# The decays of a group's scan computed at the end of the round before, in a decoder block on one core

## The chip, the cores and the metric

The kernel runs on one core of one Trainium2 chip. The metric is the device time of one execution in microseconds (us); smaller is better. Before the change three runs gave 1035.84, 1035.08 and 1036.63 us, median 1035.84.

## The reference

One layer of a hybrid decoder on 512 tokens with 16 learned meta tokens ahead of them, width 1024, in float32. A large input projection feeds two branches, a causal pooling and a Mamba-2 state-space scan (SSD). Sigmoid gates merge them, an output projection and a squared-ReLU MLP follow. The change lies in the scan, which has 8 groups of 4 heads and chunks of 128 positions:

```python
a_cs = jnp.cumsum(a_dt, axis=2)
diff = a_cs[:, :, :, None] - a_cs[:, :, None, :]
lmat = jnp.exp(jnp.where(mask, diff, -jnp.inf))
cb = jnp.einsum("bclgn,bcsgn->bclsg", cf, bf)
y_diag = jnp.einsum("bclsg,bclsgr,bcsgrp->bclgrp", cb, lmat, xdt)
...
y_off = jnp.einsum("bclgn,bcgrpn,bclgr->bclgrp", cf, prev, jnp.exp(a_cs))
...
y = y.reshape(bsz, seqlen, D_INNER) * jax.nn.silu(z)
yg = yg * lax.rsqrt(jnp.mean(yg * yg, axis=-1, keepdims=True) + EPS)
```

The "decays" are the two exponentials: `exp(a_cs)` (tile `eb`) and `lmat` (computed in place in tile `abc`, also called `dm`). The norm in the last line needs the sum of the squares of `y` (tile `sqg`).

## The kernel before, in words

Weights come in blocks of 128x1024 floats. Each is loaded by SyncE into `raw` (3 buffers), cast by ScalarE (ACT) to a rounded `whi` (L75) and completed by VectorE (DVE) with `wlo`, the rest (L76; 4 buffers each); every product is then three matmuls on TensorE (PE). Blocks are made two ahead of their use.

The scan goes in rounds g = 0 to 7. Round g runs `ssd(g)` (L398) and, between its parts, as filler for PE, the projections of group g+1 (`group_proj`, L364): `bt`, `ct`, two halves `xc`, in some rounds a gate (`pgp`, L537), and two halves of `z` (`pz`). `weave` (L524) interleaves the two by counts; PE's order is what this writing gives, while the order on ACT, DVE and the DMA queues is made by a scheduler. All engines take their instructions strictly in the order that results.

A round in PE's order, with the default counts: transposes of the group (`ptb`, `ptm`, `ptx`, L413 to L434); projection `bt`; `pcb` and the chunk states `pst` (L461 to L470); projection `ct`; projection of the first `xc`; the outputs `po` and `py` (L485, L491), called **the end of py** below; projection of the second `xc`; gate and both `pz`; the norm's column sums `png` (L508). In round 3 `STEPS` puts `png` ahead of `pz`. Round 4 has as filler first the eight half tiles `pso` of the output product (`out_half`, L569), each copied to `acc` by ACT (L574); two halves share a PSUM tile, and the second half's first matmul waits for the copy of the first. Round 7's filler is `psp` (`out_part`, L577), which needs group 6's normed rows `yh`, `yl` (L519, L520).

What ACT and DVE do for a round: the decays. POOL issues the load of `abc` (L406: four rows of `acs_d` sent to all 128 partitions, 1 MB), as soon as the `py` of the round before has read the single `abc` buffer. Then ACT makes two `eb` (L445: exp of half the partitions each), eight Relu of `abc` (L450) while DVE makes eight differences (L453), and ACT two exponentials of 128x1024 (L455, L456). Further: copies of the transposes to `btok`, `bm` (L415 to L420), and for each projection ACT's first convolution tap (L344), three taps on DVE (L347) and a Silu on ACT (L349); only the taps release the projection's PSUM tile, of which there are two (`psum2`). Then `yt` on DVE (L495 to L499), its square on ACT (L503, `sqg`, which shares the buffer of `eb`), a sum on DVE, `qhg` on ACT (L246) and `qlg` on DVE (L247) for `png`, Ln and Exp on ACT (L511, L512), the scaled rows (L516) and their split `yh`, `yl`. ACT holds one table of functions at a time: a change between Exp, Silu, Sigmoid and Ln puts an ACT_TABLE_LOAD into its order.

Of the kernel before, what the change touches and what calls it, by code (L numbers as in the profile page):

```python
# [9 lines left out]
F32 = mybir.dt.float32  # L10
F32R = mybir.dt.float32r
AF = mybir.ActivationFunctionType
ALU = mybir.AluOpType

P = 128
D = 1024
SEQ = 512
# [4 lines left out]
G = 8  # L22
R = 4
# [28 lines left out]
def kernel(ctx: ExitStack, tc, xT, x, w, vec, fnw, out):  # L52
    nc = tc.nc
    act, dve, pe, pool = nc.scalar, nc.vector, nc.tensor, nc.gpsimd
# [66 lines left out]
    dtok = const.tile([P, 2, 4, HEADS], F32, name="dtok")  # L121
# [16 lines left out]
    for i in range(2):  # L138
        dve.tensor_scalar(xm[:, 2 * i : 2 * i + 2, :].rearrange("p r d -> p (r d)"), ones_f[:MQ], 0.0, None,
                          op0=ALU.mult)  # L140
# [6 lines left out]
    def psum1(name):  # L147
        return psb.tile([P, 512], F32, tag="s", name=name)
# [93 lines left out]
    def col_sums(name, qt, n2, tags, bufs=1):  # L242

        qh = n2.tile(list(qt.shape), F32R, tag=tags[0], name=f"qh{name}", bufs=bufs)
        ql = n2.tile(list(qt.shape), F32R, tag=tags[1], name=f"ql{name}", bufs=bufs)
        act.copy(qh, qt)  # L246
        dve.tensor_tensor(ql, qt, qh.bitcast(F32), op=ALU.subtract)  # L247
        return qh, ql
# [20 lines left out]
    for i in range(2):  # L269
        pb = psum1(f"pb1_{i}")  # L270
        c = slice(3 * i, 3 * i + 3)
# [14 lines left out]
    for c in range(4):  # L286
        r = slice(c * H, (c + 1) * H)
# [23 lines left out]
    acs_d = dram.tile([H, SEQ], F32, name="acs_d")  # L311
# [39 lines left out]
    def group_tiles(g):  # L351
        xc = gc.tile([P, 2, L], F32, tag="xc", name=f"xc{g}")
        bt = gc.tile([P, L], F32, tag="bt", name=f"bt{g}")
        ct = gc.tile([P, SEQ], F32, tag="ct", name=f"ct{g}")
        zt = gc.tile([P, 2, SEQ], F32, tag="zt", name=f"zt{g}", bufs=1)
        return xc, bt, ct, zt
# [7 lines left out]
    def group_proj(g, cur, gate=None):  # L364

        first = g == 0
        xc, bt, ct, zt = cur
        for dst, t, skip in ((bt, 16 + g, 0), (ct, 24 + g, NM - 4), (xc[:, 0, :], 2 * g, 0),
                             (xc[:, 1, :], 2 * g + 1, 0)):
            if first and dst is bt:  # L370
                view = viewB
            else:
                runs, view = wide(psum2(f"px{g}_{t}"), skip)
                proj(runs, block(), X if first else U)
            conv(dst, first_raw(t, view, skip) if first else view, t)
            yield
        if gate is not None:
            gate_pool(gate)
            yield
        ps = psum2(f"pz{g}")  # L380
        for i in range(2):
            proj(narrow(ps[:, i * SEQ : (i + 1) * SEQ]), block(), X if first else U)
            if gate is None and i == 0:
                yield
        zf = zt.rearrange("p i t -> p (i t)")
        if first:
            dve.tensor_tensor(zt, ps.rearrange("p (i t) -> p i t", i=2),
                              rsb[:, NM:].unsqueeze(1).to_broadcast([P, 2, SEQ]), op=ALU.mult)
            act.activation(zf, zf, AF.Silu)
        else:  # L390
            act.activation(zf, ps, AF.Silu)
        yield


    def bc(ap, n):
        return ap.unsqueeze(len(ap.shape)).to_broadcast(list(ap.shape) + [n])

    def ssd(g, cur):  # L398

        xc, bt, ct, zt = cur  # L400
        hs = slice(R * g, R * g + R)
        tok = lambda c: slice(NM + c * P, NM + (c + 1) * P)
        ctok = lambda c: slice(c * P, (c + 1) * P)
        flat = lambda t: t.rearrange("p r d -> p (r d)")
        abc = gs.tile([P, R, SEQ], F32, tag="abc", name=f"abc{g}")
        nc.gpsimd.dma_start(abc, acs_d[hs, :].partition_broadcast(P))  # L406

        xdt = gs.tile([P, 4, R, 64], F32, tag="xdt", name=f"xdt{g}")
        xdm = gs.tile([NM, R, 64], F32, tag="xdm", name=f"xdm{g}")
        btok = gs.tile([P, 3, P], F32, tag="btok", name=f"btok{g}")  # L410
# [27 lines left out]
        xdd = gs.tile([P, 3, R, 64], F32, tag="xdd", name=f"xdd{g}")  # L438
        dve.tensor_tensor(xdd, xdt[:, :3, :, :], bc(dec[:, :3, hs], 64), op=ALU.mult)

        eb = gs.tile([P, 2, SEQ], F32, tag="eb", name=f"eb{g}")
        ap = abc.rearrange("p (i j) l -> p i j l", j=2)
        for j in range(2):
            js = slice(64 * j, 64 * j + 64)
            act.activation(eb[js, :, :], ap[js, :, j, :], AF.Exp)  # L445
        dm = abc.rearrange("p r (c l) -> p r c l", c=4)
        for r in range(R):
            for c in range(4):
                if r < 2:
                    act.activation(dm[:, r, c, :], dm[:, r, c, :], AF.Relu, scale=-1.0,  # L450
                                   bias=dtok[:, 1, c, R * g + r : R * g + r + 1])
                else:
                    dve.tensor_scalar(dm[:, r, c, :], dm[:, r, c, :], dtok[:, 1, c, R * g + r : R * g + r + 1],  # L453
                                      0.0, op0=ALU.subtract, op1=ALU.min)
        act.activation(abc[:, :2], abc[:, :2], AF.Exp, scale=-1.0)  # L455
        act.activation(abc[:, 2:], abc[:, 2:], AF.Exp)  # L456
        yield

        pc = psum1(f"pcb{g}")
# [27 lines left out]
        for i in range(2):  # L487
            for c in range(4):
                for j in range(2):
                    r = 2 * i + j  # L490
                    pe.matmul(py[i][64 * j : 64 * j + 64, c * P : (c + 1) * P],  # L491
                              xdt[:, c, r, :], dm[:, r, c, :], start=True, stop=True)
        for i in range(2):
# [4 lines left out]
                                     op0=ALU.mult, op1=ALU.add)  # L498
            dve.tensor_tensor(y, y, zt[:, i, :], op=ALU.mult)  # L499
            if i == 0:  # L500
                yield
        sq = gs.tile([P, 2, SEQ], F32, tag="eb", name=f"sqg{g}")
        act.activation(sq, yt, AF.Square)  # L503
        dve.tensor_tensor(sq[:, 0, :], sq[:, 0, :], sq[:, 1, :], op=ALU.add)
        qh, ql = col_sums(f"g{g}", sq[:, 0, :], gs, ("qh", "ql"))
        yield
        pn = psum1(f"png{g}")
        pe.matmul(pn, ones_r, qh, start=True, stop=False)  # L508
# [15 lines left out]
    def weave(a, b, counts):  # L524

        end = object()
        for _, n in zip(a, counts):
            while n and b:
                if next(b[0], end) is end:
                    b.pop(0)  # L530
                else:
                    n -= 1
        for rest in [a] + b:
            for _ in rest:
                pass
# [18 lines left out]
    gs = gc_stack.enter_context(tc.tile_pool(name="gs", bufs=1, side="left", reuse_waits="tile"))  # L554
# [14 lines left out]
    def out_half():  # L569
        for dd in range(4):  # L570
            ps = psum2(f"pso{dd}")
            for i in range(2):
                ssd_out(2 * dd + i, ps[:, i * SEQ : (i + 1) * SEQ], range(8))
                act.copy(acc[2 * dd + i], ps[:, i * SEQ : (i + 1) * SEQ])  # L574
                yield

    def out_part():  # L577

        un = units()
        for d in range(NK):  # L580
            ps = psum2(f"psp{d}")[:, :SEQ]
            for k in range(8, 14):
                mm3(ps, next(un), ys[k], k == 8, k == 13)
            dve.tensor_tensor(acc[d], acc[d], ps, op=ALU.add)
            yield

    STEPS = {3: (1, 1, 1, 1, 1, 1, 0), 4: (2, 2, 2, 2, 2, 4, 0), 7: (2, 2, 0, 2, 1, 1, 0)}
    depth[0] = 2
    with tc.manual_schedule(engines={mybir.EngineType.PE}):
        for g in range(G):  # L590
            nxt = group_tiles(g + 1) if g + 1 < G else None
            fill = [group_proj(g + 1, nxt, GATE_AT.get(g))] if nxt else [out_part()]
            if g == 4:
                fill = [out_half()] + fill
            weave(ssd(g, cur), fill, STEPS.get(g, (1, 1, 1, 1, 2, 0, 0)))
            cur = nxt
# [161 lines left out]
    for n, d in enumerate(MERGE):  # L758
# [8 lines left out]
        for i, k in enumerate(ks):  # L767
            c = slice(k * P, (k + 1) * P)
# [294 lines left out]
    c = NC - 1  # L1063
# [5 lines left out]
    for t in range(4):  # L1069
        T, st = t // 2, slice((t % 2) * P, (t % 2 + 1) * P)  # L1070
        n = 0
        for half in range(2):
            parts = [(0, 512)] if half == 0 or t < 3 else [(0, 256), (256, 256)]
            for a, m in parts:
# [3 lines left out]
                i = 0  # L1078
                for k, seg in ((1, (A11, 3)[T]), (0, (A12, A22)[T])):
                    wh, wl = wq[k, half]  # L1080
                    for p in range(2):
                        x0 = p * 512 + a
                        f = i == 0 and not (T == 0 and half == 0)
# [152 lines left out]
```

## Time and profile before

| | |
|---|---|
| median of 3 runs | 1035.84 us |
| the profiled execution, its own time | 1034.4 us |
| its span, first to last instruction | 1032.7 us |
| PE busy | 1007.3 us (98%) |
| DVE busy | 714.5 us (69%) |
| ACT busy | 562.7 us (54%) |
| mean granted TensorE clock | 0.993 |

A row of the timeline gives start and duration in us, engine, line, operation and tiles; in brackets stands the idle time of the engine before it and whose end released it. "PEclk" is the share of the full TensorE clock that was granted.

### The profile page before, as it was taken

The page shows a single profiled execution, that of the slowest core. Times are in us where ns is not written, and L with a number is a line of the kernel's source. Part 1 is how long each engine was busy: PE and PEld are TensorE (multiplying, and loading weights), DVE is VectorE, ACT ScalarE, POOL GpSimd, SP SyncE. Part 2 cuts the span into 40 slices and gives each one's busy share as a digit, 9 for nine tenths or more (in the row PEclk, how much of TensorE's full clock was granted, in tenths as well). Part 3 has the DMA queues.
Part 4 walks back from the last instruction along what each step waited for, and adds up shares of the span by engine and source line. Part 5 has one row for each costly group of instructions (what it writes and reads, how often), then busy time and mean ns, then how long its engine had stood idle before and what let it go on. Part 6 is the DMA issues. An engine that isn't in the chain of part 4 may idle for free.

```text
span 1032.7 us, 14079 instructions
## 1 busy us (share of the span) xinstructions
PE 1007.3 (98%) x5689; PEld 874.0 (85%) x5689; DVE 714.5 (69%) x950; ACT 562.7 (54%) x748; POOL 88.6 (9%) x52
## 2 busy tenths in 40 slices
PE   9999999999889999989999999999999999999997
PEld 8888889898678898968899888888888888888886
DVE  7988676776535585967756457875777567666866
ACT  7774959577526629582334333374554345454444
POOL 0100000000000000000000000002131422403400
PEclk9999999999899999999999999999999999999999
DMA  6243141423322231413532333324323323233112
GB/s 236 73 156 105 34 148 41 144 62 128 97 76 109 87 118 42 144 37 106 205 102 83 104 100 100 125 82 146 100 82 122 105 92 110 102 103 123 41 42 82
DMA packets 29281, 105.62 MB, mean 102 GB/s; under 512 B 3296, under 2 KB 4256, under 8 KB 28192
## 3 DMA queue, kind: packets, MB, share of 16 engines
q1 hardware_dynamic: 26496, 92.75, 27.7%
q0 software_dynamic: 2000, 11.08, 2.8%
q8 instruction: 44, 0.72, 0.3%
q10 hardware_dynamic: 720, 0.91, 0.3%
q14 instruction: 21, 0.17, 0.1%
HBM read 102.55 MB, written 2.16 MB: 101 GB/s over the span
## 4 chain that ended last, share of the span: by engine, by line
PE 82%; ACT 9%; DVE 6%; issue 2%; DMA 1%; SPq 0%; ACTq 0%; DVEq 0%
PE pf L96 6%; PE pf L98 6%; PE pf L97 6%; PE px L154 4%; PE px L155 4%; PE px L157 4%; PE alpha L985 3%; PE alpha L987 3%; PE alpha L986 3%; PE pz L154 2%; PE pz L157 2%; PE pz L155 2%; PE pp L157 1%; PE pp L154 1%; PE pp L155 1%
## 5 line engine op out<-in xcount | busy, mean ns | idle before, releaser
L76 DVE TENSOR_TENSOR wlo<-raw,whi 128x1024 fp32r<-128x1024 f32 (+1 forms) x131 | 163.3, 1252 | 146.8 <-ACT whi L75 146.8
L75 ACT CAST whi<-raw 128x1024 fp32r<-128x1024 f32 (+1 forms) x131 | 135.7, 1043 | 219.2 <-PE pf L97 55.8
L154 PE MATMUL px<-uh,whi 128*128 128x264 f32 (+1 forms) x448 | 120.2, 289 | 4.1 <-DVE bt L347 2.5
L155 PE MATMUL px<-ul,whi 128*128 128x264 f32 (+1 forms) x448 | 117.3, 283 | 0.0
L96 PE MATMUL pf<-vh,whi 128*128 128x512 f32 x256 | 99.8, 390 | 0.0
L98 PE MATMUL pf<-vh,wlo 128*128 128x512 f32 x256 | 99.6, 389 | 0.0
L97 PE MATMUL pf<-vl,whi 128*128 128x512 f32 x256 | 99.6, 389 | 0.0
L157 PE MATMUL px<-uh,wlo 128*128 128x264 f32 (+1 forms) x448 | 90.4, 283 | 0.0
L154 PEld LDWEIGHTS px<-uh,whi 128*128 128x128 f32 x448 | 84.7, 189 | 5.7 <-issue 3.7
L155 PEld LDWEIGHTS px<-ul,whi 128*128 128x128 f32 x448 | 84.4, 188 | 0.2
L747 DVE TENSOR_TENSOR slo<-b,shi 128x1024 fp32r<-128x1024 f32 x35 | 49.2, 1404 | 31.6 <-ACT shi L746 31.6
L157 PEld LDWEIGHTS px<-uh,wlo 128*128 128x128 f32 x448 | 68.8, 188 | 0.0
L746 ACT CAST shi<-b 128x1024 fp32r<-128x1024 f32 x35 | 36.8, 1050 | 47.3 <-PE pf L97 36.4
L98 PEld LDWEIGHTS pf<-vh,wlo 128*128 128x128 f32 x256 | 48.1, 188 | 10.0
L97 PEld LDWEIGHTS pf<-vl,whi 128*128 128x128 f32 x256 | 48.1, 188 | 10.0
L96 PEld LDWEIGHTS pf<-vh,whi 128*128 128x128 f32 x256 | 48.1, 188 | 9.8
L996 POOL TENSOR_TENSOR b<-b,b 128x1024 f32<-128x1024 f32 x14 | 35.5, 2539 | 238.3 <-DVE slo L747 238.3
L985 PE MATMUL alpha<-shi,hh 128*128 128x512 f32 x140 | 54.6, 390 | 0.0
L987 PE MATMUL alpha<-shi,hl 128*128 128x512 f32 x140 | 54.5, 389 | 0.0
L986 PE MATMUL alpha<-slo,hh 128*128 128x512 f32 x140 | 54.5, 389 | 0.0
L812 DVE TENSOR_TENSOR ht<-ht,alpha 128x1024 f32<-128x1024 f32 x35 | 42.6, 1217 | 10.9 <-PE alpha L987 10.9
L154 PE MATMUL pz<-uh,whi 128*128 128x512 f32 x112 | 44.0, 392 | 1.8 <-DVE xc L347 1.4
(419 smaller groups left out, 2497.8 us busy)
## 6 DMA issues: line engine op xcount, KB each, us to landing
raw<-in_w SPq DMA_DIRECT2D x129, 512.0 KB, 3.5
b<-in_w SPq DMA_DIRECT2D x28, 512.0 KB, 3.5
abc<-acs_d POOLq DMA_DIRECT2D x8, 1024.0 KB, 5.6
wob<-in_w SPq DMA_DIRECT2D x8, 512.0 KB, 5.2
xt<-in_xT SPq DMA_DIRECT2D x8, 264.0 KB, 5.9
ht<-in_x POOLq DMA_DIRECT2D x4, 512.0 KB, 6.2
w<-in_w SPq DMA_DIRECT2D x4, 512.0 KB, 3.5
out_dram<-out SPq DMA_DIRECT2D x4, 320.0 KB, 2.4
```

The lines of the kernel that those rows point to most:

```text
L75: act.copy(hi[:, c], raw[:, c])
L76: dve.tensor_tensor(lo[:, c], raw[:, c], hi[:, c].bitcast(F32), op=ALU.subtract)
L96: pe.matmul(ps, ah, bh, start=first, stop=False)
L97: pe.matmul(ps, ah, bl, start=False, stop=False)
L98: pe.matmul(ps, al, bh, start=False, stop=last)
L154: pe.matmul(o, wh, rhs[0][k][:, c], start=k == 0, stop=False)
L155: pe.matmul(o, wh, rhs[1][k][:, c], start=False, stop=False)
L157: pe.matmul(o, wl, rhs[0][k][:, c], start=False, stop=k == NK - 1)
L747: dve.tensor_tensor(lo, src, hi.bitcast(F32), op=ALU.subtract)
L985: pe.matmul(ps[t], a[0], wh[:, cs], start=f, stop=False, skip_group_check=True)
L986: pe.matmul(ps[t], a[0], wl[:, cs], start=False, stop=False, skip_group_check=True)
L987: pe.matmul(ps[t], a[1], wh[:, cs], start=False, stop=l, skip_group_check=True)
```

## The change

Five edits. The decays get a function of their own, `decays(g)`: load, `eb`, differences, exponentials. Group 0's are called ahead of the rounds. Those of group g+1 are called in round g after the norm's squares and `col_sums`, ahead of `png`; before, they stood in round g+1 between the transposes and `pcb`. The squares `sqg` get a buffer of their own, `sq`, so that `eb` of the next group can be written while they are in use. `STEPS` has a new entry for round 6, which puts `png` between the two halves of `pz`.

```diff
+    decay = {}
+    def decays(g):
+        hs = slice(R * g, R * g + R)
+        abc = gs.tile([P, R, SEQ], F32, tag="abc", name=f"abc{g}")
+        nc.gpsimd.dma_start(abc, acs_d[hs, :].partition_broadcast(P))
+        dm = abc.rearrange("p r (c l) -> p r c l", c=4)
+        eb = gs.tile([P, 2, SEQ], F32, tag="eb", name=f"eb{g}")
...
+        act.activation(abc[:, :2], abc[:, :2], AF.Exp, scale=-1.0)
+        act.activation(abc[:, 2:], abc[:, 2:], AF.Exp)
+        decay[g] = eb, dm
+
     def ssd(g, cur):
...
-        abc = gs.tile([P, R, SEQ], F32, tag="abc", name=f"abc{g}")
-        nc.gpsimd.dma_start(abc, acs_d[hs, :].partition_broadcast(P))
-
+        eb, dm = decay.pop(g)
...
-        eb = gs.tile([P, 2, SEQ], F32, tag="eb", name=f"eb{g}")
...
-        act.activation(abc[:, :2], abc[:, :2], AF.Exp, scale=-1.0)
-        act.activation(abc[:, 2:], abc[:, 2:], AF.Exp)
         yield
...
-        sq = gs.tile([P, 2, SEQ], F32, tag="eb", name=f"sqg{g}")
+        sq = gs.tile([P, 2, SEQ], F32, tag="sq", name=f"sqg{g}")
         act.activation(sq, yt, AF.Square)
         dve.tensor_tensor(sq[:, 0, :], sq[:, 0, :], sq[:, 1, :], op=ALU.add)
         qh, ql = col_sums(f"g{g}", sq[:, 0, :], gs, ("qh", "ql"))
+        if g + 1 < G:
+            decays(g + 1)
         yield
...
-    STEPS = {3: (1, 1, 1, 1, 1, 1, 0), 4: (2, 2, 2, 2, 2, 4, 0), 7: (2, 2, 0, 2, 1, 1, 0)}
+    STEPS = {3: (1, 1, 1, 1, 1, 1, 0), 4: (2, 2, 2, 2, 2, 4, 0), 6: (1, 1, 1, 1, 1, 1, 0), 7: (2, 2, 0, 2, 1, 1, 0)}
     depth[0] = 2
+    decays(0)
```

The lines left out are the `eb` loop and the differences, moved unchanged. How the order on the engines moves is shown at three places; the numbers behind a tile's name are the group and a running number.

Place 1: ACT, from the rounded copies of the transposes to the first tap of `bt2` in round 1. Before:

```order
L418 COPY bm_114<-ptb1_1290 16x128
L419 COPY bm_114<-ptb1_1290 16x128
L450 ACTIVATE abc1_1285<-abc1_1285,dtok_87 128x128 x2
L519 COPY yh0_0_1272<-yt0_1099 128x512
L450 ACTIVATE abc1_1285<-abc1_1285,dtok_87 128x128
L519 COPY yh0_1_1277<-yt0_1099 128x512
L450 ACTIVATE abc1_1285<-abc1_1285,dtok_87 128x128 x5
L456 ACTIVATE abc1_1285<-abc1_1285 128x1024
L455 ACTIVATE abc1_1285<-abc1_1285 128x1024
L75 COPY whi18_1343<-raw18_1342 128x1024
L344 ACTIVATE bt2_1282<-px2_18_1341,vs_85 128x528
```

The same stretch of ACT with the change:

```order
L441 COPY bm_114<-ptb1_1311 16x128
L442 COPY bm_114<-ptb1_1311 16x128
L75 COPY whi18_1343<-raw18_1342 128x1024
L528 COPY yh0_0_1295<-yt0_1099 128x512
L528 COPY yh0_1_1300<-yt0_1099 128x512
L344 ACTIVATE bt2_1305<-px2_18_1341,vs_85 128x528
```

Eight Relu and two exponentials of `abc1` have left this stretch; they now stand at the end of round 0, ahead of `whi17` and of the Silu of `zt1`.

Place 2: ACT at the end of round 3 and the start of round 4, up to the copy `acc0` of the first half tile of `pso0`. Before:

```order
L419 COPY bm_114<-ptb4_2727 16x128
L450 ACTIVATE abc4_2722<-abc4_2722,dtok_87 128x128 x5
L75 COPY whi39_2780<-raw39_2779 128x1024
L455 ACT_TABLE_LOAD
L455 ACTIVATE abc4_2722<-abc4_2722 128x1024
L456 ACTIVATE abc4_2722<-abc4_2722 128x1024
L574 COPY acc0_812<-pso0_2778 128x512
```

The same stretch with the change:

```order
L528 COPY yh3_0_2732<-yt3_2504 128x512
L528 COPY yh3_1_2737<-yt3_2504 128x512
L438 COPY btok4_2747<-ptb4_2748 128x384
L441 COPY bm_114<-ptb4_2748 16x128
L442 COPY bm_114<-ptb4_2748 16x128
L75 COPY whi39_2780<-raw39_2779 128x1024
L75 COPY whi40_2811<-raw40_2810 128x1024
L583 COPY acc0_812<-pso0_2778 128x512
```

The exponentials have moved up into round 3, and the cast of `whi40` has come ahead of `acc0`. At the end of round 4 the copy `acc6` (half tile of `pso3`) stood behind the square `sqg4` and `qhg4`; now it stands behind `sqg4`, a table load and the first `eb5`, and ahead of `qhg4`.

Place 3: ACT at the end of round 6, from group 7's decays to `yh6_0`, for which `psp` waits. Before:

```order
L445 ACT_TABLE_LOAD
L445 ACTIVATE eb7_4378<-abc7_4343 64x1024
L391 ACT_TABLE_LOAD
L391 ACTIVATE zt7_3899<-pz7_4265 128x1024
L511 ACT_TABLE_LOAD
L511 ACTIVATE rs6_4330<-png6_4327,eps_83 128x512
L415 COPY btok7_4347<-ptb7_4348 128x384
L512 ACT_TABLE_LOAD
L512 ACTIVATE rs6_4330<-rs6_4330 128x512
L418 COPY bm_114<-ptb7_4348 16x128
L450 ACTIVATE abc7_4343<-abc7_4343,dtok_87 128x128 x2
L519 COPY yh6_0_4334<-yt6_4161 128x512
```

The same stretch with the change:

```order
L420 ACT_TABLE_LOAD
L420 ACTIVATE abc7_4265<-abc7_4265 128x1024
L419 ACTIVATE abc7_4265<-abc7_4265 128x1024
L520 ACT_TABLE_LOAD
L520 ACTIVATE rs6_4322<-png6_4319,eps_83 128x512
L75 COPY whi65_4326<-raw65_4325 128x1024
L521 ACT_TABLE_LOAD
L521 ACTIVATE rs6_4322<-rs6_4322 128x512
L391 ACT_TABLE_LOAD
L391 ACTIVATE zt7_3922<-pz7_4288 128x1024
L528 COPY yh6_0_4357<-yt6_4161 128x512
```

The rest of the Relu, both exponentials and the cast of `whi65` now stand ahead of `yh6_0`, and the small copies of `ptb7` behind it. In rounds 0 to 3, 5 and 6 the first `eb` of the next group, which waits for the load of `abc`, now stands on ACT ahead of the first tap of the second `xc` and of the square `sqg`; before, it stood behind `qhg`. PE's order differs in round 6 alone, where the two matmuls of `png6` stand ahead of the second half of `pz7`.

More of the change, by code (lines that the diff above doesn't have):

```diff
@@ L396, in bc @@
         return ap.unsqueeze(len(ap.shape)).to_broadcast(list(ap.shape) + [n])
+    decay = {}
[5 more added lines that the diff above has]
+        eb = gs.tile([P, 2, SEQ], F32, tag="eb", name=f"eb{g}")
+        ap = abc.rearrange("p (i j) l -> p i j l", j=2)
+        for j in range(2):
+            js = slice(64 * j, 64 * j + 64)
+            act.activation(eb[js, :, :], ap[js, :, j, :], AF.Exp)
+        for r in range(R):
+            for c in range(4):
+                if r < 2:
+                    act.activation(dm[:, r, c, :], dm[:, r, c, :], AF.Relu, scale=-1.0,
+                                   bias=dtok[:, 1, c, R * g + r : R * g + r + 1])
+                else:
+                    dve.tensor_scalar(dm[:, r, c, :], dm[:, r, c, :], dtok[:, 1, c, R * g + r : R * g + r + 1],
+                                      0.0, op0=ALU.subtract, op1=ALU.min)
+        act.activation(abc[:, :2], abc[:, :2], AF.Exp, scale=-1.0)
+        act.activation(abc[:, 2:], abc[:, 2:], AF.Exp)
+        decay[g] = eb, dm
     def ssd(g, cur):
@@ L439, in ssd @@
         dve.tensor_tensor(xdd, xdt[:, :3, :, :], bc(dec[:, :3, hs], 64), op=ALU.mult)
-        eb = gs.tile([P, 2, SEQ], F32, tag="eb", name=f"eb{g}")
[L442 to L456, printed above, removed]
         yield
```

## The prediction

> **What bounds it now.** I read the page first: PE is nearly always busy, and the chain that ended last lies on it for 82%.
>
> ```profile
> span 1032.7 us, 14079 instructions
> ...
> PE 1007.3 (98%) x5689; PEld 874.0 (85%) x5689; DVE 714.5 (69%) x950; ACT 562.7 (54%) x748; POOL 88.6 (9%) x52
> ...
> PE 82%; ACT 9%; DVE 6%; issue 2%; DMA 1%; SPq 0%; ACTq 0%; DVEq 0%
> ```
>
> The change removes no work from PE, so what it can win are PE's pauses, 1032.7 - 1007.3 = 25 us at most, part of it at both ends of the run. Next I read PE's list of waits (engine, line, whom it waits for: total, times, longest):
>
> ```profile
> PE pso L96 <- ACT acc L574: 7.5, 4, 4.1
> PE psp L96 <- ACT yh L519: 3.2, 1, 3.2
> ```
>
> and the rows of PE where a pause ends (beside a `pst` and a `pz` that are used further down):
>
> ```profile
> 119.44 0.37 PE L468 MATMUL pst<-xm,bm 80*128 80x256 f32 x1
> ...
> 129.30 0.36 PE L154 MATMUL px<-uh,whi 128*128 128x264 f32 x1 [2.48 <-DVE bt L347]
> ...
> 269.65 0.80 PE L96 MATMUL pso<-yh,whi 128*128 128x512 f32 x1 [4.08 <-ACT acc L574]
> ...
> 436.37 0.40 PE L154 MATMUL pz<-uh,whi 128*128 128x512 f32 x1
> ...
> 455.71 0.79 PE L96 MATMUL psp<-yh,whi 128*128 128x512 f32 x1 [3.21 <-ACT yh L519]
> ```
>
> All three long ones are late work of ACT or of what follows it, and each is near a group's decays: in round 1, at the start of round 4 and at the start of round 7. The pauses cost more than their length. In the windows of the three pauses and behind two of them (length, PE busy, PEld, DVE, ACT, POOL, granted clock, DMA share, GB/s) the clock is 0.50 after the two longer ones:
>
> ```profile
> 126.80:129.30 2.50, 0.02 (x2) 0.03 (x1) 2.50 (x6) 0.85 (x2) 0.00 (x0) 1.00 0.67 197
> ...
> 264.50:268.00 3.50, 1.07 (x5) 0.56 (x3) 1.89 (x3) 3.47 (x5) 0.00 (x0) 1.00 0.00 0
> 268.00:271.40 3.40, 1.75 (x4) 1.46 (x5) 0.82 (x1) 3.40 (x5) 0.00 (x0) 0.50 0.57 154
> 271.40:274.80 3.40, 3.40 (x9) 2.63 (x9) 1.53 (x2) 0.09 (x1) 0.00 (x0) 0.50 0.49 153
> ...
> 455.70:459.10 3.40, 3.33 (x7) 2.35 (x8) 1.46 (x4) 3.40 (x9) 0.00 (x0) 0.50 0.00 0
> ```
>
> After the pause of 4.08 PE does 1.75 + 3.40 us of work at half speed, which loses 2.6; after that of 3.21 it loses 3.33 / 2 = 1.7; in that of 2.48 it stays 1.00, and no row behind it shows less, so nothing.
>
> **When the load of abc lands** decides the change, since `eb` now heads ACT's order. The load itself is not moved: POOL issues it as soon as `py` has released the buffer.
>
> ```profile
> 94.08 0.53 POOL L406 DMA_DIRECT2D abc<-acs_d  x1 [42.96 <-PE py L491]
> ...
> 236.30 0.53 POOL L406 DMA_DIRECT2D abc<-acs_d  x1 [47.83 <-DVE xc L347]
> 309.47 0.53 POOL L406 DMA_DIRECT2D abc<-acs_d  x1 [72.64 <-DVE yt L496]
> ...
> 431.05 0.53 POOL L406 DMA_DIRECT2D abc<-acs_d  x1 [47.86 <-DVE yt L495]
> ```
>
> From issue to landing it took, in rounds 5, 3 and 6 in this order:
>
> ```profile
> abc<-acs_d POOLq DMA_DIRECT2D x1, 1024.0 KB, 5.2
> ...
> abc<-acs_d POOLq DMA_DIRECT2D x1, 1024.0 KB, 6.0
> ...
> abc<-acs_d POOLq DMA_DIRECT2D x1, 1024.0 KB, 7.2
> ```
>
> In rounds 3 and 6 weight loads were ahead of it on the same DMA engines. The change casts weights earlier in the `ct` part of a round, so one load fewer stands in the way there; I take 5.2 for rounds 0 and 4 and 5.5 for rounds 3 and 6, nearer to the first row, and keep 7.2 as the far end.
>
> **The change part by part.** Rows of ACT around the pause of round 1, two of DVE behind them:
>
> ```profile
> 99.58 1.05 ACT L75 CAST whi<-raw 128x1024 fp32r<-128x1024 f32 x1 [3.44 <-PE px L155]
> ...
> 103.84 1.28 ACT L445 ACT_TABLE_LOAD   x1
> 105.14 1.06 ACT L445 ACTIVATE eb<-abc 64x1024 f32<-64x1024 f32 x1
> ...
> 119.54 1.56 ACT L450 ACTIVATE abc<-abc,dtok 128x128 f32<-128x128 f32 x5
> 121.01 1.04 ACT L456 ACTIVATE abc<-abc 128x1024 f32<-128x1024 f32 x1
> 121.96 1.04 ACT L455 ACTIVATE abc<-abc 128x1024 f32<-128x1024 f32 x1
> ...
> 123.84 0.78 ACT L344 ACTIVATE bt<-px,vs 128x528 f32<-128x528 f32 x1
> ```
>
> ```profile
> 118.66 0.28 DVE L420 TENSOR_TENSOR bm<-ptb,bm 16x128 fp32r<-16x128 f32 x1
> ...
> 128.39 0.76 DVE L347 SCALAR_TENSOR_TENSOR bt<-px,vs,bt 128x525 f32<-128x525 f32 x1
> ```
>
> *A, the pause of 2.48.* PE waits for the third tap of `bt`, which ends at 129.15, because the first tap stands behind the decays. These leave (some 4 us), two `yh` come ahead, so the tap starts 2 to 3 us earlier and the pause is gone. What is late next: the decays, now in round 0, push `zt` and `bm` back. Added ahead of `bm` are eight Relu (0.31 each by the row of five, 2.5) and two exponentials (1.9, their starts lie 0.95 apart). Taken away are one table load (the first Exp table loads while ACT waits for the landing, 1.28) and ACT's wait for the sum of squares (0.93, by the row of `qhg` below). The start is 94.08 + 5.2 + 0.1 = 99.4 in place of 99.58. That makes 2.5 + 1.9 - 1.28 - 0.93 - 0.2 = 2.0, less some 0.5 for rows that overlap by 0.1: `bm` ends near 120.4 in place of 118.94, and `pst`, which started at 119.44, waits 1.0. **A = -2.48 + 1.0 = -1.5**, with bounds 0 (a new wait of the same length) and -2.5.
>
> In rounds 1, 2 and 5 nothing is won or lost: the gate and both `pz` give PE 16 us more before it needs the norm, and no pause stands there now.
>
> ```profile
> 241.57 1.05 ACT L75 CAST whi<-raw 128x1024 fp32r<-128x1024 f32 x1 [2.33 <-PE px L155]
> ...
> 245.20 0.62 ACT L246 CAST qhg<-sqg 128x512 fp32r<-128x512 f32 x1 [0.93 <-DVE sqg L504]
> ...
> 269.03 0.56 ACT L574 COPY acc<-pso 128x512 f32<-128x512 f32 x1
> ```
>
> *B, the pause of 4.08.* From 241.57 to `acc0` at 269.03 ACT is full, 27.46 us, and the same rows stand there afterwards in another order. They start at 236.30 + 5.5 + 0.1 = 241.9, lose the 0.93 and one table load of 1.28, and gain the cast of `whi40` (0.95): `acc0` at 268.1. **B = -0.9**; landing at 7.2 would give +0.8, at 4.8 -1.6.
>
> *C, the clock after it.* PE then pauses 4.08 - 0.9 = 3.2, of which some 0.5, an estimate from the length of a `yh` and its `yl`, lies apart and earlier, since `yl3` comes late to the first half tile. The rest, 2.7, lies between 2.48 (clock kept) and 3.21 (clock halved), nearer to the first. **C = -2.6**; the other end is 0.
>
> The Trainium skill ("TensorE: Matmul & The Clock Gate", section "HAM oscillation — how this bites in real kernels") gives the rule that PE must not idle for over about 3.4 us. The trace does not hold to it: the pause of 3.21 was enough. By that rule C would be sure; by the row it is not.
>
> *D, the new place of acc6.*
>
> ```profile
> 312.31 1.06 ACT L503 ACTIVATE sqg<-yt 128x1024 f32<-128x1024 f32 x1 [5.73 <-DVE yt L499]
> ...
> 314.65 0.58 ACT L574 COPY acc<-pso 128x512 f32<-128x512 f32 x1
> ```
>
> Afterwards a table load and one `eb` stand between them: 313.37 + 1.28 + 1.06 = 315.7 (the load lands at 309.47 + 5.2 = 314.7, no later than the table). PE already waits for this copy: **D = +1.1**. The later `acc7` has slack, since `bt5` needs another PSUM tile.
>
> *E, the pause of 3.21.*
>
> ```profile
> 436.32 1.05 ACT L75 CAST whi<-raw 128x1024 fp32r<-128x1024 f32 x1 [1.50 <-PE px L155]
> ...
> 440.05 0.62 ACT L246 CAST qhg<-sqg 128x512 fp32r<-128x512 f32 x1 [1.03 <-DVE sqg L504]
> ...
> 451.61 0.47 ACT L415 COPY btok<-ptb 128x384 f32<-128x384 f32 x1
> ...
> 455.05 0.60 ACT L519 CAST yh<-yt 128x512 fp32r<-128x512 f32 x1
> ```
>
> From 436.32 to `yh` are 18.73 us. Taken away: the wait of 1.03, one table load, `btok` (0.47) and the two smaller `bm` (as much together); added: six Relu (1.9) and two exponentials (1.9), together +0.5. The start is 431.05 + 5.5 + 0.1 = 436.65, so `yh` comes 0.8 later: **E = +0.8**, at 7.2 +2.5, at 4.8 +0.1. The half clock behind it stays. That `png6` moves up costs nothing: a stall there would be taken out of the same pause.
>
> The Trainium skill ("ScalarE: Activation LUTs", section "What ACT_TABLE_LOAD costs") adds a drain of about 1.38 us to each table load. The trace shows `eb` at 105.14, 0.02 after the load's end; by the page's price B and E would each be 1.4 better, by the row they stand as above.
>
> *Sum:* -1.5 - 0.9 - 2.6 + 1.1 + 0.8 = -3.1, hence 1034.4 - 3.1 = 1031.3 for an execution like the profiled one. That one lies 1.4 under the median of the runs, 1035.84; beside the median the forecast is **1032.7**.
>
> **The rivals.**
>
> *The clock does not hold.* The shorter pause still halves it (C = 0): -0.5, 1035.3. For it: the two pauses that did so differ by only 0.9 us, and the one that remains is just under the shorter. Against it: 2.48 did not.
>
> *Slower: ACT waits for the landing.* ACT takes its rows in order, so taps and squares queue behind an `eb` whose data is not there. At 7.2 in all rounds: E +2.5, B +0.8, C 0, D 309.47 + 7.2 + 0.1 + 1.06 - 314.65 = +3.2, A some +0.5, and in rounds 1, 2 and 5 `pz` waits about 0.7 each for the taps of the second `xc` (from issue to landing 7.2, then `eb`, a first tap, the sum and three taps, 4.5 by rows of their kind; `pz` in round 6 starts 436.37 - 431.05 = 5.3 after the issue, and the gate ahead of it in these rounds takes one projection more, about as much again and 0.4). Sum +9.1, 1044.9. It decides from about 5.8 on, where the terms cancel without C. For it: the 6.0 and 7.2. Against it: the weight loads that caused them move.
>
> *The wait is replaced.* The pause of round 1 becomes one of the same length at `pst` (A = 0): 1034.2. The order speaks for some of it (the two new casts on DVE ahead of `bm`), the ledger above for less than half.
>
> **How the numbers follow.** Forecast 0.45; clock 0.30; late landing 0.15; replaced wait 0.10. The forecast's own range is 1031 to 1034. The low end of all, 1029.8, takes landing at 4.8 (B and E 1.4 better) and the half clock after E gone with it (1.7); the high end, 1037.8, leaves out the worse part of the late landing. A measurement can tell 0.2%, 2.1 us, from no change. Faster by more: the forecast and a bit of the others, 0.50; within: the clock, the replaced wait and the forecast's upper edge, 0.33; slower: 0.17.
>
> **What would show it.** A: no pause of `px` on `bt`, and one of about 1 us at `pst` in round 1. B and C: the pause at the first `pso` near 3 us, and a clock of 1.00 behind it. D: the third wait of `pso` on `acc` near 1.75. E: `psp` waits 4 us. The prediction is wrong if `abc` lands over 5.8 after its issue, if the clock is halved three times, or if a wait stands in rounds 1, 2 or 5.

## The result, and the profile after

The change makes the kernel slower. Four runs gave 1044.10 to 1049.48 us, median 1046.96; the median of the kernel before, run beside them, is 1035.46. The ratio is 1.0112, with a 95% interval of 1.0082 to 1.0142. The forecast was 1032.7, the highest bound that it gave 1037.8; 1046.96 lies above both. The profiled execution took 1047.11, its span is 1044.7.

From the page after: span, busy times, and shares of the chain that ended last.

```profile
span 1044.7 us, 14089 instructions
...
PE 1009.3 (97%) x5689; PEld 874.8 (84%) x5689; DVE 714.0 (68%) x950; ACT 563.4 (54%) x749; POOL 88.7 (8%) x52
...
PE 80%; ACT 10%; DVE 5%; DMA 3%; issue 1%; SPq 0%; ACTq 0%; POOLq 0%; DVEq 0%
```

PE is busy 2.0 us longer; the other engines work as much as before, to within 0.8. The span is 12.0 longer, so some 10 are pauses of PE. In the chain, DMA has gone from 1% to 3%: transfers now end last where they did not. PE's waits after (engine, line, whom it waits for: total, times, longest):

```profile
PE pso L96 <- ACT acc L583: 5.2, 4, 1.7
PE pst L475 <- DVE bm L443: 5.0, 1, 5.0
PE ptx L457 <- DVE xdm L447: 3.9, 3, 1.3
PE png L517 <- ACT qhg L246: 3.8, 2, 2.2
PE pz L154 <- DVE xc L347: 3.5, 3, 1.6
PE psp L96 <- ACT yh L528: 2.3, 1, 2.3
...
PE ptx L457 <- ACT rs L520: 1.3, 1, 1.3
PE png L518 <- DVE qlg L247: 0.5, 2, 0.2
```

Before, the list held `pso` 7.5, `psp` 3.2 and, of those that change,

```profile
PE px L154 <- DVE bt L347: 2.5, 1, 2.5
...
PE pz L154 <- DVE xc L347: 1.4, 1, 1.4
```

So `pst` adds 5.0, `ptx` 3.9 + 1.3, `png` 3.8 + 0.5 and `pz` 2.1, which is 16.6; `px` gives back 2.5, `pso` 2.3 and `psp` 0.7 (a later wait of 0.2 counted), which is 5.5. The balance is +11.1; the small pauses together are about 1 shorter. Of the 2.0 us more of PE, about 1.1 is work at half clock: 8.5 us were done at it before and 10.7 with the change, and half of that is lost. For the rest no row here gives a cause.

Where do these waits come from? ACT at the end of round 0 (start, duration; in brackets the idle time before and whose end released it):

```profile
94.94 0.65 ACT L349 ACTIVATE xc<-xc 128x528 f32<-128x528 f32 x1 [3.88 <-DVE xc L347]
101.34 1.28 ACT L410 ACT_TABLE_LOAD   x1 [5.76 <-DMA abc<-acs_d]
102.64 1.06 ACT L410 ACTIVATE eb<-abc 64x1024 f32<-64x1024 f32 x1
103.61 0.77 ACT L344 ACTIVATE xc<-px,vs 128x528 f32<-128x528 f32 x1
104.28 1.05 ACT L510 ACTIVATE sqg<-yt 128x1024 f32<-128x1024 f32 x1
...
116.93 1.03 ACT L391 ACTIVATE zt<-pz 128x1024 f32<-128x1024 f32 x1
...
122.42 0.25 ACT L442 CAST bm<-ptb 16x128 fp32r<-16x128 f32 x1
```

ACT stands idle for 5.76 us, and what ends it is the landing of `abc`. Only then comes the table load, 1.28, then `eb`, and behind these the tap of the second `xc` and the square. In round 6 the same stands at 446.21, after 4.04 us. From issue to landing the load took, in rounds 0 and 6 (4.5, 6.3, 6.1, 5.0 and 5.2 in rounds 1 to 5):

```profile
abc<-acs_d POOLq DMA_DIRECT2D x1, 1024.0 KB, 7.8
...
abc<-acs_d POOLq DMA_DIRECT2D x1, 1024.0 KB, 6.7
```

The `ptx` waits are another thing. ACT in round 1 and then DVE in the same stretch:

```profile
159.33 1.06 ACT L420 ACTIVATE abc<-abc 128x1024 f32<-128x1024 f32 x1
160.30 1.04 ACT L419 ACTIVATE abc<-abc 128x1024 f32<-128x1024 f32 x1
...
163.24 2.93 ACT L75 CAST whi<-raw 128x1024 fp32r<-128x1024 f32 x3
```

```profile
164.31 3.50 DVE L76 TENSOR_TENSOR wlo<-raw,whi 128x1024 fp32r<-128x1024 f32 x3 [8.70 <-ACT whi L75]
167.72 0.41 DVE L447 TENSOR_TENSOR xdm<-ptm,decm 16x256 f32<-16x256 f32 x1
```

Three casts of weights stand on ACT behind the exponentials and the gate. DVE has three `wlo` next in its order, idles 8.70 us for the first cast, and only then makes `xdm`, whose PSUM bank the next transposes need: 1.3 us of pause at the end of each of rounds 1, 2 and 5.

The clock (length of the stretch, PE busy, PEld, DVE, ACT, POOL, granted clock, DMA share, GB/s), in and behind the pause of `pst`, then behind `png` of round 3 and `psp`:

```profile
121.20:124.20 3.00, 0.02 (x1) 0.06 (x1) 1.83 (x4) 2.95 (x7) 0.00 (x0) 0.50 0.00 0
124.60:128.00 3.40, 3.40 (x12) 2.86 (x12) 3.40 (x6) 3.14 (x5) 0.00 (x0) 0.50 0.44 139
...
257.70:261.10 3.40, 3.40 (x10) 2.62 (x9) 0.00 (x0) 3.37 (x8) 0.00 (x0) 0.50 0.00 0
...
469.30:472.70 3.40, 3.40 (x10) 2.63 (x9) 3.40 (x4) 2.32 (x3) 0.00 (x0) 0.50 0.16 22
```

It is halved three times, 13.7 us in all, in place of twice and 10.2.

### The profile page after: what moved, and what is told of

It reads as the page before. It is cut to its first block, busy times and chain, and to the rows that moved or that the text cites. A ratio compares the mean times of both kernels' runs of the same rounds, so it can differ in the third digit from the quotient of the medians.

```text
span 1044.7 us, 14089 instructions
## 1 busy us (share of the span) xinstructions
PE 1009.3 (97%) x5689; PEld 874.8 (84%) x5689; DVE 714.0 (68%) x950; ACT 563.4 (54%) x749; POOL 88.7 (8%) x52
## 4 chain that ended last, share of the span: by engine, by line
PE 80%; ACT 10%; DVE 5%; DMA 3%; issue 1%; SPq 0%; ACTq 0%; POOLq 0%; DVEq 0%
PE pf L96 6%; PE pf L98 6%; PE pf L97 6%; PE px L154 4%; PE px L155 4%; PE px L157 4%; DMA abc<-acs_d 3%; PE alpha L995 3%; PE alpha L997 3%; PE alpha L996 3%; PE pp L154 1%; PE pp L157 1%; PE pp L155 1%; PE pgs L157 1%; PE pup L98 1%; PE pgs L154 1%
```

## The experiments

Two theories stood at first. **Landing**: time is lost because the first `eb` and its table load stand ahead of tap and square, and wait for `abc`. **Place**: time is lost because all the decays are written at the end of the round. The first four runs:

*The buffer alone*, on the kernel before:

```diff
-        sq = gs.tile([P, 2, SEQ], F32, tag="eb", name=f"sqg{g}")
+        sq = gs.tile([P, 2, SEQ], F32, tag="sq", name=f"sqg{g}")
```

> The kernel before with one edit: the squares of the norm get a buffer of their own; the decays stay where they were written. Landing theory: in the changed kernel time is lost because the first eb and the table load ahead of it stand on ACT ahead of the first tap of the second xc and of the square, and both wait for the landing of abc. The order of this kernel shows the same there (the shared buffer had held eb behind the square), so it is slow although nothing was moved by hand: pauses of pz on xc and of pst on bm as with the whole change, 1041 to 1045. Place theory: time is lost because the decays are written at the end of the round, so Relu, exponentials and casts of weights come in another order; then the buffer alone does nothing, 1034 to 1037.

Measured: 1046.58, ratio 1.0107 (1.0091 to 1.0123). The smallest edit of the five, alone, costs as much as the whole change, and more than either theory had. The waits are the landing's kind (`png` 4.1, `pst` 3.7, `pz` 3.7, `psp` 6.9). The shared buffer had been a brake on the scheduler (the planner, in the texts on record): with it `eb` cannot be written before the square has been read.

*The place alone*, on the changed kernel:

```diff
-        sq = gs.tile([P, 2, SEQ], F32, tag="sq", name=f"sqg{g}")
+        sq = gs.tile([P, 2, SEQ], F32, tag="eb", name=f"sqg{g}")
```

> The whole change, but the squares share the buffer of eb again. The first eb then stands on ACT behind the square and qhg, as before the change. Landing theory: no tap and no square waits for a landing, the pauses of pz and png go, that of pst in round 1 falls below 2, and the pause of px on bt stays away as with the change: 1033 to 1037. Place theory: the decays stay at the end of the round with all their rows ahead of the casts, so most of the loss stays: 1042 to 1047.

Measured: 1045.40, ratio 1.0089 (1.0076 to 1.0102). The landing theory fell here as the only cause. No tap waits for a landing in this kernel, and it is still 10 us slow. PE's waits:

```profile
PE psp L96 <- ACT yh L528: 7.8, 1, 7.8
PE pst L475 <- DVE bm L443: 6.4, 4, 3.8
```

ACT in round 6 of this kernel, from the cast that starts its full stretch to `yh`:

```profile
442.44 1.05 ACT L75 CAST whi<-raw 128x1024 fp32r<-128x1024 f32 x1 [4.21 <-PE px L155]
...
453.40 2.45 ACT L414 ACTIVATE abc<-abc,dtok 128x128 f32<-128x128 f32 x8
455.76 1.05 ACT L420 ACTIVATE abc<-abc 128x1024 f32<-128x1024 f32 x1
456.71 1.04 ACT L419 ACTIVATE abc<-abc 128x1024 f32<-128x1024 f32 x1
...
465.78 1.13 ACT L528 CAST yh<-yt 128x512 fp32r<-128x512 f32 x2
```

From cast to `yh` are 23.34 us, before 18.73: 4.6 more, which is just what `psp` waits more (7.8 for 3.2). The rows that came ahead are as long: six Relu (1.9), two exponentials (1.9) and one cast (1.0) are 4.8, less some overlap.

*The table ahead of time, first try*, on the changed kernel (an exponential whose result nothing uses is added):

```diff
+        wt = gs.tile([P, 1], F32, tag="wt", name=f"wt{g}")
+        act.activation(wt, eps, AF.Exp)
         for j in range(2):
```

> The whole change, with one exponential of a single element ahead of the first eb, on data that is always there. The table load then takes place while ACT waits for the landing, 1.28 earlier. Landing theory: whatever stands behind the first eb comes 1.28 earlier, so each of the pauses pst in round 1, ptx in rounds 1, 2, 5 and 6, pz in round 2, png in rounds 3 and 6 and psp shrinks by up to 1.3, about 10 in all: 1036 to 1040. Rival, that these pauses come from the rows between eb and the casts, or from the landing alone with slack behind it: under 3 us, 1044 to 1047.

Measured: 1046.83. It tells nothing of the table: the added row waits for nothing, and the scheduler put all eight at the start of round 0. From there on ACT's order is that of the changed kernel, so this run is a repeat of it.

*Two buffers for `abc`*, on the changed kernel; its load is then issued a round earlier:

```diff
-        abc = gs.tile([P, R, SEQ], F32, tag="abc", name=f"abc{g}")
+        abc = gs.tile([P, R, SEQ], F32, tag="abc", name=f"abc{g}", bufs=2)
...
-        sq = gs.tile([P, 2, SEQ], F32, tag="sq", name=f"sqg{g}")
+        sq = gs.tile([P, 2, SEQ], F32, tag="xdt", name=f"sqg{g}")
```

> The whole change, with two buffers for abc, so that its load is issued a round earlier and has landed long before eb; for room the squares use the buffer of xdt. Landing theory: eb then waits only for DVE's reading of the old eb, some 4 us earlier than the landing; ptx, pz and png pauses go, pst in round 1 falls to about 1 with no half clock behind it: 1029 to 1035. Place theory: the rows stand in nearly the same order on ACT, with the three casts behind the exponentials, so ptx and pst pauses stay and only some of pz and png goes: 1040 to 1045.

Measured: **1024.34**, ratio 0.9890 (0.9876 to 0.9903): faster than both kernels, and below what either theory had. ACT in round 0 of this kernel:

```profile
95.28 0.65 ACT L349 ACTIVATE xc<-xc 128x528 f32<-128x528 f32 x1 [3.87 <-DVE xc L347]
95.94 1.28 ACT L410 ACT_TABLE_LOAD   x1
97.24 2.14 ACT L410 ACTIVATE eb<-abc 64x1024 f32<-64x1024 f32 x2
99.61 0.79 ACT L344 ACTIVATE xc<-px,vs 128x528 f32<-128x528 f32 x1 [0.23 <-PE px L157]
...
117.23 0.26 ACT L442 CAST bm<-ptb 16x128 fp32r<-16x128 f32 x1
```

The table load and both `eb` fill the time in which ACT would wait for `px`; the tap still waits 0.23 for PE, so they cost nothing. `bm` ends at 117.5, as early as before the change (117.6), though all Relu and exponentials now lie ahead of it, and 5.2 earlier than with the change. The list of PE's waits holds no `pst`, `ptx`, `png` or `px` on `bt`:

```profile
PE pso L96 <- ACT acc L583: 5.0, 4, 1.5
PE psp L96 <- ACT yh L528: 2.0, 1, 2.0
```

From these four came a third theory, **budget**: from the end of `py` to `bm`, `yh` and `acc` ACT has no free time, so a decay row that comes ahead of these costs its length, unless it fills ACT's idle time ahead of the end of `py`. That needs an early landing and an order that does not hold `eb` back. Four more runs:

*Two buffers on the kernel before*, one line:

```diff
-        abc = gs.tile([P, R, SEQ], F32, tag="abc", name=f"abc{g}")
+        abc = gs.tile([P, R, SEQ], F32, tag="abc", name=f"abc{g}", bufs=2)
```

> The kernel before with two buffers for abc and nothing else, so its load is issued a round earlier; ACT and DVE keep their order. Budget theory (formed after the first four runs): from the end of py to bm, yh and the copies acc ACT has no free time, so decay rows that stand ahead of these cost their length, unless they fill ACT's idle time ahead of the end of py; that needs both an early landing and an order in which eb is not held behind the square. Here eb is still held behind the square by the shared buffer: no gain, 1034 to 1037. Rival, that the early load itself is what made the kernel with two loads fast (a DMA queue freed for the weights): 1024 to 1030.

Measured: 1034.85, ratio 0.9999 (0.9989 to 1.0010). The rows of PE, ACT and DVE stand in the same order as in the kernel before, so this holds the order fixed: an early load by itself is worth nothing.

*Two buffers, squares back in the buffer of `eb`*, on the changed kernel:

```diff
-        abc = gs.tile([P, R, SEQ], F32, tag="abc", name=f"abc{g}")
+        abc = gs.tile([P, R, SEQ], F32, tag="abc", name=f"abc{g}", bufs=2)
...
-        sq = gs.tile([P, 2, SEQ], F32, tag="sq", name=f"sqg{g}")
+        sq = gs.tile([P, 2, SEQ], F32, tag="eb", name=f"sqg{g}")
```

> The whole change with two buffers for abc, and with the squares sharing the buffer of eb. ACT's order is that of the whole change with the shared buffer (1045.4). Budget theory: eb is held behind the square although its data lies there, no idle time is filled, and all Relu and exponentials stand ahead of bm and yh: 1043 to 1047, with psp waiting over 6. Rival, that the landing alone decides: 1024 to 1035.

Measured: 1045.51, ratio 1.0095 (1.0082 to 1.0108), `psp` 7.8. The rows of the three engines stand in the order of the kernel with one load (1045.40). The data lies there, but the order holds it back; nothing is won.

*Two buffers, decays in their old place*, on the kernel before (with its `STEPS`):

```diff
-        abc = gs.tile([P, R, SEQ], F32, tag="abc", name=f"abc{g}")
+        abc = gs.tile([P, R, SEQ], F32, tag="abc", name=f"abc{g}", bufs=2)
...
-        sq = gs.tile([P, 2, SEQ], F32, tag="eb", name=f"sqg{g}")
+        sq = gs.tile([P, 2, SEQ], F32, tag="xdt", name=f"sqg{g}")
```

> The kernel before with two buffers for abc, and the squares in the buffer of xdt, so that eb is no longer held behind them; the decays stay where they were written and STEPS is the old one. Budget theory: the order on ACT comes out nearly as with the whole change and two loads (both eb ahead of the tap), so the place where the decays are written is worth little: 1023 to 1028. Rival, that the place is what pays once the load is early: 1031 to 1036.

Measured: 1031.26, ratio 0.9962 (0.9950 to 0.9974). This missed the budget theory's 1023 to 1028 and fell into the rival's range; the theory gave too little to the place: `psp` waits 4.0 and `ptx` 2.8 where the kernel with the new place has 2.0 and none.

*The table ahead of time, again*, on the changed kernel (again with a result that nothing uses); `ready` is a column of `yt`:

```diff
+        if g:
+            wt = gs.tile([P, 1], F32, tag="wt", name=f"wt{g}")
+            act.activation(wt, ready, AF.Exp, scale=0.0)
         for j in range(2):
```

> The whole change, with one exponential of one column of yt (scaled by zero, so a one) ahead of the first eb of rounds 0 to 6; it keeps its place directly ahead of eb, which the first try did not, since that one had nothing to wait for and all eight went to the start of round 0. The table is then loaded while ACT waits for the landing. Budget theory: everything behind eb comes up to 1.28 earlier, so pst in round 1 pauses 3.8 in place of 5.0, ptx, pz and png pauses nearly go, psp falls to about 1: 1036 to 1042. Rival, that the table load is not in the way: 1045 to 1048.

Measured: 1038.69, ratio 1.0041 (1.0025 to 1.0057): 8.3 us less than the whole change. ACT in round 0:

```profile
95.73 1.28 ACT L410 ACT_TABLE_LOAD   x1
97.03 0.20 ACT L410 ACTIVATE wt<-yt 128x1 f32<-128x1 f32 x1
99.50 1.06 ACT L413 ACTIVATE eb<-abc 64x1024 f32<-64x1024 f32 x1 [2.27 <-DMA abc<-acs_d]
```

The load of the table now lies in the idle time, and `eb` starts at the landing. The pause at `pst` is gone altogether, that of `png` fell from 3.8 to 0.6; `psp` stayed at 2.3, which the theory had at 1, and a `ptx` pause of 2.3 is new at the end of round 0. In this execution `abc` landed early in round 0, 5.8 after its issue; it did so in the first try too (6.2, the table load at 100.05), and that kernel took 1046.83. So an early landing in round 0 does not explain the 8.1 between the two tries. But not all of it need be the table's: four casts of weights on ACT and some `wlo` and taps on DVE also changed places, and in other rounds `abc` landed up to 0.8 earlier (7.0 for 7.8 in round 2).

What stayed open then was the share of `STEPS`, and two controls. The last four:

*Two buffers, old `STEPS`*, on the kernel with 1024.34:

```diff
-    STEPS = {3: (1, 1, 1, 1, 1, 1, 0), 4: (2, 2, 2, 2, 2, 4, 0), 6: (1, 1, 1, 1, 1, 1, 0), 7: (2, 2, 0, 2, 1, 1, 0)}
+    STEPS = {3: (1, 1, 1, 1, 1, 1, 0), 4: (2, 2, 2, 2, 2, 4, 0), 7: (2, 2, 0, 2, 1, 1, 0)}
```

> The whole change with two loads (squares in the buffer of xdt; 1024.34), but without the new entry of STEPS for round 6, so png6 stands behind both halves of pz7 again. It lies between that kernel and the one with the decays in their old place (1031.26), which differ in this entry too. If the entry is what shortened the wait of psp from 3.95 to 2.00 and kept the clock, this takes back that part: psp waits 3 to 5, the clock is halved behind it once, 1026 to 1030. If the place of the decays did it: psp stays near 2, 1023.5 to 1025.5.

Measured: 1027.10, ratio 0.9925 (0.9912 to 0.9937), `psp` 3.6 and 0.8 more on `yl`. So the entry is worth 2.8 here, and of the 6.9 between old and new place 4.2 are the place's.

*The squares in the buffer of `xdt`, one buffer for `abc`*, on the changed kernel:

```diff
-        sq = gs.tile([P, 2, SEQ], F32, tag="sq", name=f"sqg{g}")
+        sq = gs.tile([P, 2, SEQ], F32, tag="xdt", name=f"sqg{g}")
```

> The whole change with one buffer for abc, its squares in the buffer of xdt in place of one of their own. A control for the kernel with two loads, which differs from this in the second buffer alone. Budget theory: 1045 to 1048, the same pauses as with the whole change. Rival, that the place of the squares made the kernel with two loads fast: below 1040.

Measured: 1048.01, ratio 1.0128 (1.0113 to 1.0142). The rows of PE, ACT and DVE stand in the order of the whole change. Where the squares lie does not matter as long as it is not with `eb`; the second buffer of `abc` is what brings 1024.34.

*The whole change without the new entry of `STEPS`* (the same diff as two above, on the changed kernel):

> The whole change without the new entry of STEPS for round 6. The pause of png in round 6 (2.2 and 0.2) goes. If that pause is taken out of the one that psp has afterwards, as the prediction said, psp waits about 2 longer than 2.3 and the time stays, 1045.5 to 1048.5. If png6 cost by itself: 1043 to 1045.

Measured: 1049.81, ratio 1.0151 (1.0123 to 1.0179). Both expectations were too low. `png` of round 6 no longer waits, but `psp` waits 9.2 in place of 2.3: without the entry the Ln for `rs6` starts at 464.93 in place of 460.85, behind the Silu of `zt`, and `yh6` at 469.32 in place of 466.65. The interval overlaps that of the whole change (up to 1.0142); the pair with two loads, where it does not, shows the same 2.8.

*Two buffers, the load held back*, on the kernel with 1024.34 (`ready` is 16 columns of `yt`; the load overwrites what POOL writes):

```diff
+        if g:
+            pool.tensor_tensor(abc[:, 0, :16], ready, ready, op=ALU.add)
         nc.gpsimd.dma_start(abc, acs_d[hs, :].partition_broadcast(P))
```

> The whole change with two buffers for abc and the squares in that of xdt (1024.34), but POOL writes 16 columns of the new abc from yt ahead of each load (the load overwrites them), so the load is issued at the end of py, as with one buffer, or a little later. The planner knows of the late landing and puts the first eb behind the square. If the time of the landing is what counts, no idle time of ACT is filled: 1042 to 1048. If a second buffer by itself is what counts: 1024 to 1030.

Measured: 1044.01, ratio 1.0090 (1.0070 to 1.0109), with `psp` waiting 6.0 and `ptx` 4.6. A second buffer without the early landing brings nothing like 1024. Since the scheduler also changed the order, the run does not part the late landing from the order that follows from it.

The medians side by side, in us:

| | `eb` held behind the square | squares elsewhere |
|---|---|---|
| one load, old place | 1035.46 | 1046.58 |
| one load, new place and `STEPS` | 1045.40 | 1046.96 |
| two loads, old place | 1034.85 | 1031.26 |
| two loads, new place and `STEPS` | 1045.51 | **1024.34** |

The edits do not add up: the buffer costs 11.1 alone and 1.6 on top of the place, where the two intervals overlap. With two loads the same buffer wins 3.6 in the old place and 21.2 in the new one.

## Why the prediction was wrong

*What failed first* is a term that stands in A, B and E: "the first Exp table loads while ACT waits for the landing, 1.28". The row at 101.34 shows the table load starting only behind the landing, so ACT's full stretch kept it; the same holds in rounds 3 and 6, for B and E. The run with the table ahead is 8.3 us faster over the kernel, though some other rows moved in it too. In round 4 alone, where D lies, the table was loaded ahead of the landing as forecast. One step was right in kind and wrong in size, the landing: 5.2 taken for rounds 0 and 4, 5.5 for rounds 3 and 6, where 7.8, 5.0, 6.1 and 6.7 were measured. The hope that one weight load fewer would stand in the way did not show.

*A.* The pause of `px` on `bt` went, as said. At `pst` 1.0 was forecast and 5.04 came. The row of ACT's second `bm` before the change:

```profile
117.33 0.26 ACT L419 CAST bm<-ptb 16x128 fp32r<-16x128 f32 x1
```

It ended at 117.59, and with the change at 122.67: 5.1 later, where 1.5 was forecast. Of the 3.6 between, 3.2 are there from the start: `eb` was to begin at 99.4 and began at 102.64 (1.9 for the landing, 1.3 for the table). A came out as +2.6 in place of -1.5, and the clock halved in that pause.

*Rounds 1, 2 and 5*, "nothing is won or lost", is the step that was wrong in kind. It looked at the norm alone and left out two things that wait behind ACT's rows: DVE's `wlo`, which hold back `xdm` (`ptx`, 3.9), and the taps (`pz`, 2.1). Together they are 6.0, more than any other term.

*B and C.* The first `pso` went from 4.08 to 0.79, 3.3 less where 0.9 less was forecast, and the half clock behind it is gone, as C had it. That is luck: the pause of 2.7 on which C was argued never came, since the time had been lost ahead of it. `png` of round 3, which no term held, waits 1.57 and 0.22, with a half clock behind. That pause, and one of 2.0 in the kernel with two loads, are shorter than 2.48 and halved the clock all the same, so C's step from the length of a pause does not hold.

*D* was right: +1.1 forecast, the wait went from 0.68 to 1.66, +1.0.

*E.* `psp` waits 2.3, less than the 4 forecast, but `png6` (2.2 and 0.2) and the `ptx` behind it (1.3) came ahead: 6.2 for 3.2. "That `png6` moves up costs nothing" was too cautious: the entry saves 2.8 us in the pair with two loads; in the pair with one load it is 2.9, with intervals that overlap.

*The rival* "slower: ACT waits for the landing" named the mechanism and came to 1044.9, but half of its terms lie elsewhere than it put them; it had +2.5 at E and +3.2 at D, and nothing for `ptx` or `png`. Nor was the landing all: with `eb` behind the square, no wait for it and the old buffers, the new place alone gives 1045.40. Of the three signs named for a wrong prediction all came: `abc` landed later than 5.8 after its issue (in four of seven rounds), the clock was halved three times, and waits stood in rounds 1, 2 and 5. A slip without effect: the range's low end, 1029.8, comes out of its own terms as 1029.6.

What is shown: the buffer alone and the place alone each cost 10 to 11 us; a row that loads the table in the idle time takes 8 off the whole change; with an early landing and a free order the change wins 11. That the losses of buffer and place overlap because both delay the same rows of ACT is read from the traces and was not parted by a run. The order of the instructions was the same in three pairs of runs (the two early loads that won nothing, and the squares in the buffer of `xdt`); in the others the scheduler made it anew, so there an edit's price holds for the edit and the order that came of it.

## What to carry to other kernels

Ask of every instruction that is moved up what it waits for, and what is queued behind it on its engine: here work moved ahead of its data's landing blocked taps, squares and casts, and 1 MB more of SBUF for an early load, with the squares out of `eb`'s buffer, turned the same move from +11 us to -11. A buffer that two tiles share is also an order, and giving a tile its own lets a scheduler reorder more than the diff shows. And a busy share of 54% says nothing of the stretch that counts; there ACT was full, and each row put ahead cost its length.

## What the runs showed of the hardware

A table load can lose its place in the idle time although it needs no data. In round 0 ACT idled 5.76 us for `abc` and only then loaded the table for 1.28. In round 4 of the same kernel the load ran at once, while `abc`, issued at 315.20, landed 5.0 later:

```profile
319.12 1.28 ACT L410 ACT_TABLE_LOAD   x1
320.41 1.06 ACT L410 ACTIVATE eb<-abc 64x1024 f32<-64x1024 f32 x1
```

So it did in round 1 of the run with the buffer alone, where `eb` itself then waited:

```profile
145.40 1.28 ACT L445 ACT_TABLE_LOAD   x1
148.34 1.06 ACT L445 ACTIVATE eb<-abc 64x1024 f32<-64x1024 f32 x1 [1.66 <-DMA abc<-acs_d]
```

The traces tell the two cases apart. Over all runs, 36 loads of the table for an `eb` started behind the landing for which ACT idled, and each has a separate wait instruction of its own line directly ahead of it (in round 0 at 101.30); 6 ran ahead of the landing, and none of them has one. With the 36, `eb` has something else to wait for besides; with the 6, the landing alone. So the load stands behind a wait that is not its own. A one-column activation of 0.20 ahead of both, on data already there, takes the load into the idle time.

The length of a pause does not by itself decide the clock. Here are stretches of 3.41 us in the kernel before. The first two share the pause of 2.48, the third holds the start of that of 4.08:

```profile
124.64:128.05 3.41, 2.18 (x19) 1.97 (x17) 3.41 (x5) 2.92 (x4) 0.00 (x0) 1.00 0.21 29
128.05:131.47 3.42, 2.17 (x18) 2.20 (x19) 3.42 (x7) 2.23 (x3) 0.00 (x0) 1.00 0.33 129
...
264.59:268.00 3.41, 0.98 (x5) 0.48 (x3) 1.80 (x3) 3.38 (x4) 0.00 (x0) 1.00 0.00 0
```

Two of the kernel with two loads, of which the first holds a pause of 2.0 whole:

```profile
442.15:445.56 3.41, 1.41 (x7) 0.81 (x5) 2.60 (x5) 3.38 (x5) 0.00 (x0) 1.00 0.49 154
445.56:448.98 3.42, 3.30 (x8) 2.36 (x8) 3.26 (x8) 2.99 (x6) 0.00 (x0) 0.50 0.00 0
```

The pause of 2.48, split by an edge, leaves 2.2 us of work on each side, and the clock stays; that of 2.0 leaves 1.41 in one stretch, and the next is at half clock. The stretches lie on a grid: in the kernel before the half clocks start at 267.97 and 455.70, 187.73 apart, 55 times 3.413; with the change at 121.17, 257.71 and 469.33, which is 40 and 62 times. The other traces that have more than one half clock ahead of the end show the same grid. The Trainium skill ("TensorE: Matmul & The Clock Gate", section "Part 1: The HAM clock gate") tells of a free-running window of 3413 ns; the trace agrees. PE's busy time in a stretch does not sort all cases, though. Two stretches of the changed kernel:

```profile
448.86:452.27 3.41, 1.47 (x7) 0.89 (x5) 3.38 (x9) 3.36 (x6) 0.00 (x0) 1.00 0.00 0
465.93:469.34 3.41, 1.80 (x7) 1.27 (x8) 3.29 (x7) 3.37 (x7) 0.00 (x0) 1.00 0.22 91
```

Behind the first, with 1.47 of work, the clock stayed; behind the second, with 1.80, it was halved. What decides between them stays open.
